# Weight tiles at six further distances from the moving operands, within 256 bytes

## The chip, the cores and the metric

The kernel runs on one core of one Trainium2 chip. The metric is the device time of one launch in microseconds, the median of several runs. Beside it stands one profiled execution with its span, from its first to its last instruction.

## The reference

One layer of a decoder trunk over 1024 tokens of width 2048, in float32:

```
h   = rmsnorm(x) * g_pre
u   = h @ w_in                      # 2048 x 7184: q, k, v, gates of two head groups
o1  = gated linear attention, 4 heads, chunked; rmsnorm per head; * silu(gate)
o2  = stick-breaking attention, 8 heads, strictly causal; * silu(gate)
x   = x + rmsnorm(concat(o1, o2) @ w_out) * g_post
x   = x + sigmoid(x @ w_g + b_g) * (p @ w_p)
```

Nearly all of the arithmetic is in three dense products: with `w_in` (2048 x 7184), `w_out` and `w_g` (2048 x 2048 each).

## The kernel before

Everything is kept transposed: features lie on the 128 partitions, tokens along the free dimension. A dense product has a weight block of 128 x 128 as TensorE's stationary operand and 128 x 512 of activations (half the tokens) as the moving one. To be exact enough, each float32 operand is split into a high part and a low remainder (`split`: ScalarE rounds a copy, VectorE subtracts it), and each block product is three matmuls: high weights with high activations, low with high, high with low. All of these land in the same accumulator `dn` in PSUM and are issued by one helper (L101).

The *first stage* works through `w_in` in units of 128 output columns. `dense` fetches a unit's weights in four pieces with `wload`: a raw tile of 128 x 512 is loaded and split into `hi` and `lo`, from a pool `w` with four buffers for each of the two. A piece holds four blocks, used for both halves of the tokens, so it serves 4 x 2 x 3 = 24 matmuls. There are 216 pieces. Between these matmuls, pieces of the attention (the tiles s, u, X, E, st and others, with accumulators z, t and o) are put in by a list of jobs that is advanced at each step. The last ten gate units of the stage have no such jobs beside them; their results pass through tiles gu, gs, ol and oB of a pool `gates`, and are stored to `og_d`.

The *wide tiles* belong to the rest: two last gate units, then the products with `w_out` and `w_g` in a form of blocks of quarters, with sums and differences of blocks in place of some of the products. Weight tiles here are 128 x 1024: a raw tile `wr` is loaded and split by `wsplit` into `wh` and `wl`, three buffers each, in a pool `mix` that is opened where the pools `w` and `gates` are closed. A wide tile holds eight blocks and serves 8 x 3 = 24 matmuls; there are 120 of them.

The order on each engine comes from a planner that works from program order and the priorities set by `tc.high_priority`. The pools are stacked: constants, activations (`ah`, `al`, 4096 bytes each per partition), `w`, and above it the pools of the attention or the gates. A tile that lies where an older tile lay waits for that tile's last use. Small filler tiles (`gap`) stand behind the small constants, so that each weight tile and each activation tile starts at a multiple of 256 bytes within the partition. Addresses per partition: activations from 7,168, `w` from 138,240, `gates` from 158,720 with oB at 168,960 to 171,008, and in `mix` the first `wr` at 172,032.

Of the kernel before, what the change touches and what calls it, by code (L numbers as in the profile page):

```python
# [12 lines left out]
F32R = mybir.dt.float32r  # L13
# [5 lines left out]
P = 128  # L19
D = 2048  # L20
T = 1024
HT = 512
# [35 lines left out]
W = 2 * HT  # L58
# [5 lines left out]
def layer(ctx, tc, xT, w_in, w_lr, w_a2, b_a, g_pre, g_head, w_out, g_post,  # L64
# [16 lines left out]
    wpool = w_open.__enter__()  # L81
# [5 lines left out]
    def nm(base):  # L87
        serial[0] += 1
        return f"{base}_{serial[0]}"
# [21 lines left out]
    def split(hi, lo, src, eng=None):  # L111
        A.activation(hi, src, AF.Copy)  # L112
        (eng or V).tensor_tensor(lo, src, f(hi), op=ALU.subtract)  # L113
# [5 lines left out]
    turn_raw = [0]  # L119
    lo_eng = [V]  # L120

    def wload(src):
        n = src.shape[-1]
        with tc.high_priority(offset=700):
            raw = new_raw[turn_raw[0] % len(new_raw)]()
            turn_raw[0] += 1
            hi = wpool.tile([P, HT], F32R, tag="hi", name=nm("hi"))
            lo = wpool.tile([P, HT], F32R, tag="lo", name=nm("lo"))
            dma(raw[:, :n], src)
            split(hi[:, :n], lo[:, :n], raw[:, :n], lo_eng[turn_raw[0] % len(lo_eng)])  # L130
        return hi, lo
# [11 lines left out]
    def dense(wsrc, acts, halves, evac):  # L143
        out_ps = {hf: ps("dn") for hf in halves}
        for q in range(KT // 4):
            hi, lo = wload(wsrc[q])
            for kk in range(4):
                k = 4 * q + kk
                sl = slice(kk * P, (kk + 1) * P)
                for hf in halves:  # L150
                    ah, al = acts[hf][k]
                    mm(out_ps[hf], hi[:, sl], ah, k == 0, False)
                    mm(out_ps[hf], lo[:, sl], ah, False, False)
                    mm(out_ps[hf], hi[:, sl], al, False, k == KT - 1)
                if k < KT - 1:
                    step()
        for hf in halves:
            with tc.high_priority(offset=300):
                evac(hf, out_ps[hf])
        step()  # L160
# [49 lines left out]
    with tc.tile_pool(name="start", bufs=1) as sp:  # L210
# [12 lines left out]
        raws = {hf: [] for hf in HALVES}  # L223
        for q in range(4):
            w = [wload(w_in[n, q]) for n in range(2)]
            for kk in range(4):
                k = 4 * q + kk
# [512 lines left out]
    with tc.tile_pool(name="mix", bufs=1, reuse_waits="tile") as mp:  # L740
        def mt(tag, bufs, n=W, dt=F32, name=None):
            return mp.tile([P, n], dt, tag=tag, name=nm(name or tag), bufs=bufs)
# [16 lines left out]
        def staged(src):  # L759
            t = mt("ar", 3)  # L760
            dma2(t, src)
            return t
# [14 lines left out]
        def wload2(src):  # L777
            raw = mt("wr", 4)
            dma(raw, src)
            return raw  # L780

        def wsplit(raw):
            hi, lo = mt("wh", 3, dt=F32R), mt("wl", 3, dt=F32R)
            split(hi, lo, raw)
            return hi, lo

# [118 lines left out]
        for hf in (1, 0):  # L905
            if hf == 0:
                job(fill("A11", 0, plain(og_d[1])))
                job(sums_12(range(3), None, early))
            for n in range(KT - LATE_SOLO, KT):
                p = None  # L910
                for kh in HALVES:
                    with ahead():
                        raw = mt("wr", 4)
                        for q in range(2):
                            dma(part(raw, q), w_in[GATE0 + n, 2 * kh + q])
                        w = wsplit(raw)
                    p = product(x_act[hf][8 * kh:8 * kh + 8], w, p=p, last=kh == 1)
                with soon():
                    if n % 2 == 0:
                        z = mt("ev", 2)  # L920
                    V.tensor_tensor(part(z, n), p, rstd[hf], op=ALU.mult)
                    if n % 2:
                        o, g = staged(o_d[hf][n // 2]), mt("sq", 1)
                        A.activation(g, z, AF.Sigmoid)
                        V.tensor_tensor(z, z, o, op=ALU.mult)
                        V.tensor_tensor(z, z, g, op=ALU.mult)
                        dma2(og_d[hf][n // 2], z)
# [3 lines left out]
        for j in range(8):  # L931
            with ahead():
                w = wsplit(wload2(w_out[0, 0, j]))
            p = product(sets["A11"], w)
            with soon():
                A.activation(u(j), p, AF.Copy)
                if j % 2:
                    dma2(m_d[j // 2], st_u[j // 2])
# [3 lines left out]
        for j in range(8):  # L942
            with ahead():
                b11, t1, t2 = (wload2(w_out[kh, nh, j]) for kh, nh in ((0, 0), (0, 1), (1, 1)))
                sub(t1, t1, b11)
                sub(t2, t1, t2)
                w2, w1 = wsplit(t2), wsplit(t1)
                add(b11, b11, t2)
                dma(t2_d[j], t2)
                dma(t3_d[j], b11)  # L950
            p = product(sets["S2"], w2)
            with soon():
                add(u(j), p, u(j))
            p = product(sets["S1"], w1)
            with soon():
                add(v(j), p, u(j))
# [267 lines left out]
```

## Time and profile before

| | |
|---|---|
| median of 3 runs | 2147.19 us (2143.7 to 2147.61) |
| the profiled execution | 2148.85 us, its span 2147.1 us |
| TensorE busy with matmuls | 2111.7 us (98%) |
| TensorE busy with weight loads | 1746.6 us (81%) |
| VectorE, ScalarE, GpSimd busy | 1372.7, 831.1, 106.7 us |
| share of the chain that ended last: matmuls into `dn` | 67% |
| bytes moved by DMA | 300.38 MB, 140 GB/s on average |

PE in the views is TensorE with its matmuls, PEld its weight loads, which run beside them. Matmuls are pipelined, so that the length of one in the profile is longer than the time from one start to the next. "L101" is line 101 of the kernel, and "dn<-ah,hi" says that the tile dn is written from ah and hi. The chain of waits goes back from the last instruction, at each step to what released it.

### The profile page before, as it was taken

The numbers are of one execution on the slowest core, as the hardware profiler recorded it, in microseconds if no ns is written. First come the engines' busy times: TensorE is split into PE (matmuls) and PEld (weight loads), VectorE is DVE, ScalarE is ACT, GpSimd is POOL, SyncE is SP. The second block draws the span as 40 slices with busy tenths as digits, with TensorE's granted clock in tenths as the row PEclk, the third lists the DMA queues.
The fourth block names the chain that finished last, engine by engine and source line by source line (L and its number), as shares of the span: only waits on it lengthen the run. The fifth ranks groups of instructions, "written<-read, shape, count | busy, mean of one in ns | idle before, by whom it ended". The sixth has DMA issues, their size and how long they took to land.

```text
span 2147.1 us, 26863 instructions
## 1 busy us (share of the span) xinstructions
PE 2111.7 (98%) x9904; PEld 1746.6 (81%) x9904; DVE 1372.7 (64%) x2147; ACT 831.1 (39%) x1347; POOL 106.7 (5%) x228
## 2 busy tenths in 40 slices
PE   9999999999999999999999999979999999999998
PEld 6788888888888888888888888868788888778787
DVE  8557676766666666666666232336777787886665
ACT  7333333333455454544544111123233443432332
POOL 3000000000101110110110000000000000000000
PEclk9999999999999999999999999989999999999999
DMA  6222221222233333333334333258887686786663
GB/s 205 73 54 56 59 61 59 55 60 55 62 86 89 75 89 88 89 81 78 93 102 120 94 98 98 87 174 311 312 319 251 219 312 205 271 286 219 223 206 123
DMA packets 215844, 300.38 MB, mean 140 GB/s; under 512 B 122913, under 2 KB 127905, under 8 KB 215713
## 3 DMA queue, kind: packets, MB, share of 16 engines
q1 hardware_dynamic: 215712, 298.67, 44.5%
q8 instruction: 77, 1.26, 0.2%
q14 instruction: 55, 0.44, 0.1%
HBM read 215.25 MB, written 56.10 MB: 126 GB/s over the span
## 4 chain that ended last, share of the span: by engine, by line
PE 77%; DMA 10%; DVE 8%; issue 2%; ACT 2%; SPq 0%; DVEq 0%; POOL 0%; ACTq 0%
PE dn L101 67%; PE z L101 5%; DMA wr<-w_g 3%; PE t L101 2%; PE o L101 2%; DVE wl L113 2%; DMA E<-X 1%; DMA ar<-h_d 1%; DMA ar<-og_d 1%; DMA wr<-w_out 1%; DVE ev L772 1%; DVE al L113 1%; DVE wr L772 1%; ACT ah L112 0%; DMA ar<-c_d 0%
## 5 line engine op out<-in xcount | busy, mean ns | idle before, releaser
L101 PE MATMUL dn<-ah,hi 128*128 128x512 f32 x1728 | 686.2, 397 | 0.2 <-ACT u L679 0.2
L101 PE MATMUL dn<-al,hi 128*128 128x512 f32 x1728 | 674.4, 390 | 0.9 <-DVE al L238 0.9
L101 PE MATMUL dn<-ah,lo 128*128 128x512 f32 x1728 | 673.8, 390 | 0.0
L101 PE MATMUL dn<-ah,wh 128*128 128x512 f32 x960 | 375.6, 391 | 11.0 <-ACT wh L112 11.0
L101 PEld LDWEIGHTS dn<-ah,hi 128*128 128x128 f32 x1728 | 325.0, 188 | 71.5 <-issue 3.6
L101 PEld LDWEIGHTS dn<-al,hi 128*128 128x128 f32 x1728 | 324.3, 188 | 72.2 <-DVE al L238 2.6
L101 PE MATMUL dn<-ah,wl 128*128 128x512 f32 x960 | 375.4, 391 | 3.5 <-DVE wl L113 3.5
L101 PE MATMUL dn<-al,wh 128*128 128x512 f32 x960 | 374.7, 391 | 0.0
L101 PEld LDWEIGHTS dn<-ah,lo 128*128 128x128 f32 x1728 | 325.2, 188 | 60.1
L112 ACT ACTIVATE hi<-raw 128x512 fp32r<-128x512 f32 x216 | 135.6, 628 | 304.5 <-PE dn L101 301.8
L113 DVE TENSOR_TENSOR lo<-raw,hi 128x512 fp32r<-128x512 f32 x216 | 150.3, 697 | 154.9 <-ACT hi L112 154.4
L101 PEld LDWEIGHTS dn<-ah,wh 128*128 128x128 f32 x960 | 181.4, 189 | 49.8 <-ACT wh L112 11.5
L101 PEld LDWEIGHTS dn<-ah,wl 128*128 128x128 f32 x960 | 181.5, 189 | 42.3 <-DVE wl L113 4.5
L101 PEld LDWEIGHTS dn<-al,wh 128*128 128x128 f32 x960 | 181.0, 189 | 37.5
L112 ACT ACTIVATE wh<-wr 128x1024 fp32r<-128x1024 f32 x120 | 126.0, 1055 | 186.7 <-PE dn L101 116.4
L113 DVE TENSOR_TENSOR wl<-wr,wh 128x1024 fp32r<-128x1024 f32 x120 | 145.8, 1218 | 18.3 <-ACT wh L112 17.8
L320 ACT ACTIVATE X<-E 128x256 uint16<-128x256 uint16 (+2 forms) x96 | 81.0, 844 | 128.5 <-DVE E L595 117.2
L590 DVE TENSOR_TENSOR_SCAN X<-X 128x128 f32<-128x128 f32 (+2 forms) x96 | 98.1, 1021 | 37.1 <-POOL X L584 24.6
L605 DVE COPY v<-E 128x512 uint16<-128x512 uint16 (+1 forms) x160 | 63.6, 430 | 59.5 <-DMA E<-X 50.2
L112 ACT ACTIVATE ah<-ar 128x1024 fp32r<-128x1024 f32 x48 | 50.9, 1061 | 105.8 <-DVE ar L775 50.8
L113 DVE TENSOR_TENSOR s<-v,s 128x512 fp32r<-128x512 f32 (+1 forms) x82 | 52.3, 637 | 48.3 <-ACT s L112 46.4
L112 ACT ACTIVATE s<-v 128x512 fp32r<-128x512 f32 (+1 forms) x82 | 47.9, 584 | 74.6 <-DVE v L605 43.3
(208 smaller groups left out, 2178.3 us busy)
## 6 DMA issues: line engine op xcount, KB each, us to landing
raw<-w_in SPq DMA_DIRECT2D x216, 256.0 KB, 2.7
wr<-w_g SPq DMA_DIRECT2D x64, 512.0 KB, 4.4
wr<-w_out SPq DMA_DIRECT2D x56, 512.0 KB, 4.8
ar<-og_d SPq DMA_DIRECT2D x36, 512.0 KB, 5.4
ar<-h_d SPq DMA_DIRECT2D x36, 512.0 KB, 4.8
xraw<-xT SPq DMA_DIRECT2D x32, 256.0 KB, 4.4
o_d<-o SPq DMA_DIRECT2D x32, 256.0 KB, 2.0
t_d<-wr SPq DMA_DIRECT2D x16, 512.0 KB, 3.2
```

What stands on the lines that cost most here:

```text
L101: PE.matmul(o, lhsT, rhs, start=start, stop=stop)
L112: A.activation(hi, src, AF.Copy)
L113: (eng or V).tensor_tensor(lo, src, f(hi), op=ALU.subtract)
L320: A.activation(pl.rearrange("p (two n) -> p two n", two=2), src.bitcast(U16)[:, :2 * n].rearrange("p (n two) -> p two n", two=2), AF.Copy)
L590: V.tensor_tensor_scan(rev, rev, rev, initial=kq[:, n:n + 1], op0=ALU.mult, op1=ALU.bypass)
L605: V.tensor_copy(to[:, :, :m, j], w[:, :, 2 * g:2 * g + m])
L772: V.tensor_tensor(dst, a, b, op=ALU.add)
```

## The change

The weight tiles of both kinds get 64 more elements (256 bytes) per partition, and the part that is used begins some elements into the tile. In the first stage it is 24, 40, 4 and 8 elements in turn (96, 160, 16 and 32 bytes), for the wide tiles 0, 8 and 32 in turn (0, 32 and 128 bytes). The high and the low tile of a pair begin at the same offset. The activations stay where they are, so the offset is also the distance of the weights from the moving operands within 256 bytes.

```diff
         with tc.high_priority(offset=700):
             raw = new_raw[turn_raw[0] % len(new_raw)]()
             turn_raw[0] += 1
-            hi = wpool.tile([P, HT], F32R, tag="hi", name=nm("hi"))
-            lo = wpool.tile([P, HT], F32R, tag="lo", name=nm("lo"))
+            o = (8, 24, 40, 4)[turn_raw[0] % 4]
+            hi = wpool.tile([P, HT + 64], F32R, tag="hi", name=nm("hi"))[:, o:o + HT]
+            lo = wpool.tile([P, HT + 64], F32R, tag="lo", name=nm("lo"))[:, o:o + HT]
             dma(raw[:, :n], src)
...
+        turn_w = [0]
+
         def wsplit(raw):
-            hi, lo = mt("wh", 3, dt=F32R), mt("wl", 3, dt=F32R)
+            o = (0, 8, 32)[turn_w[0] % 3]
+            turn_w[0] += 1
+            hi, lo = (mt(t, 3, W + 64, F32R)[:, o:o + W] for t in ("wh", "wl"))
             split(hi, lo, raw)
             return hi, lo
```

## The prediction

> **What bounds the kernel now.** The page comes first: the span, the busy times by engine, the granted clock by slice.
>
> ```profile
> span 2147.1 us, 26863 instructions
> PE 2111.7 (98%) x9904; PEld 1746.6 (81%) x9904; DVE 1372.7 (64%) x2147; ACT 831.1 (39%) x1347; POOL 106.7 (5%) x228
> PEclk9999999999999999999999999989999999999999
> ```
>
> TensorE is busy for 98% of the span at a clock that falls in one slice only. A busy TensorE is not yet a fast one, since its matmuls overlap. So the second view is the groups of instructions with their counts and lengths:
>
> ```profile
> L101 PE MATMUL dn<-ah,hi 128*128 128x512 f32 x1728 | 686.2, 397 | 0.2 <-ACT u L679 0.2
> L101 PE MATMUL dn<-ah,wh 128*128 128x512 f32 x960 | 375.6, 391 | 11.0 <-ACT wh L112 11.0
> L101 PEld LDWEIGHTS dn<-ah,hi 128*128 128x128 f32 x1728 | 325.0, 188 | 71.5 <-issue 3.6 <-ACT ah L237 3.4 <-ACT hi L112 2.5
> L101 PE MATMUL t<-s,u 128*128 128x256 f32 x288 | 43.3, 282 | 0.0
> ```
>
> The group "ah, hi" of 1728 has two sisters of the same count (al with hi, ah with lo), so the first stage has 3 x 1728 = 5184 of these matmuls; "ah, wh" of 960 stands likewise for 3 x 960 = 2880 of the wide tiles. The sum is 8064. A length of 391 ns is not the price of one. The price is the pitch, from one start to the next, and the chain of waits gives it, where "x999" matmuls follow one another with nothing between:
>
> ```profile
> 1181.44 2.75 PE dn L101 x12
> 1184.19 0.71 PE t L101 x6
> 1184.90 226.48 PE dn L101 x999
> ```
>
> 226.48 us / 999 = 226.7 ns for 512 columns. 8064 x 226.7 ns = 1828 us, 85% of the span. The kernel is bound by this pitch, and each nanosecond of it on all 8064 is 8.1 us (0.4%). What else ends waits (loads at the borders between stages, 11 us before the first wide matmul) the change touches in one place only, told below.
>
> Two more readings say what the pitch is made of. First, the six matmuls of 256 columns above take 0.71 / 6 = 118.3 ns each, with the same 128 x 128 weight load. 512 columns cost 226.7 - 118.3 = 108.4 ns more than 256, so 512 columns stream in 216.8 ns, and 9.9 ns of each pitch go with the matmul and its weight load, not with its columns. The second is the timeline of TensorE in the first stage, just after other matmuls have come in between (columns: start us, length us):
>
> ```profile
> 303.19 0.47 PE L101 MATMUL dn<-ah,hi 128*128 128x512 f32 x1
> 303.50 0.39 PE L101 MATMUL dn<-ah,lo 128*128 128x512 f32 x1
> 303.73 0.39 PE L101 MATMUL dn<-al,hi 128*128 128x512 f32 x1
> ...
> 304.88 0.39 PE L101 MATMUL z<-E,ones_r 128*128 128x512 f32 x1
> 305.11 0.39 PE L101 MATMUL dn<-ah,hi 128*128 128x512 f32 x1
> ...
> 307.15 0.39 PE L101 MATMUL dn<-ah,hi 128*128 128x512 f32 x1
> 307.38 0.39 PE L101 MATMUL dn<-ah,lo 128*128 128x512 f32 x1
> ```
>
> From 303.50 to 305.11 are seven steps, 1.61 / 7 = 230.0 ns each; from 305.11 to 307.38 are ten, 2.27 / 10 = 227.0 ns. All of them have 512 columns and one weight load, no wait is shown, and weights and moving operands start on multiples of 256 bytes. So the pitch is no constant: after a disturbance it is 3.3 ns above the settled value, and it settles within some seven matmuls. How the stream of the moving operand and the load of the next weights lie to each other in time does count. Whether their distance in memory counts too, no row shows, for every pair of the 8064 has distance 0.
>
> **The change part by part.**
>
> *The weights' start.* In the first stage all 216 pairs of hi and lo start 96, 160, 16 or 32 bytes later, 54 pairs each, and so all 5184 matmuls get a distance they did not have. Of the 120 wide pairs a third keeps 0, a third gets 32 and a third 128: 40 x 24 = 960 matmuls stay, 1920 move. Together 7104 move. No instruction is added or removed; the price is 7104 times the change of pitch. From below the bound is the 9.9 ns: if a distance took away all that goes with the weight load, 7104 x 9.9 = 70 us would be gained. From above I take the same amount once more, 70 us lost, since a load that got in the way twice as often would cost that. Between the two I take the row nearest to a pair out of step, 230.0 ns: 7104 x 3.3 ns = 23.4 us more. The reason for that sign is that the settled 226.7 is the best stretch on the chain, and what was seen at another relation of the two streams is slower. A milder form is that each new tile disturbs the pitch and it settles again: 336 tiles, all 216 + 120, x 7 steps x 3.3 ns = 7.8 us.
>
> *The weight load itself.* It lasts 188 ns and is due every 226.7, so it has 38 ns of cover; taken at nothing. If a displaced load took over 38 ns longer, each nanosecond beyond would be 7.1 us.
>
> *The splits.* ScalarE writes hi, VectorE reads it and writes lo, now at the shifted start.
>
> ```profile
> L112 ACT ACTIVATE hi<-raw 128x512 fp32r<-128x512 f32 x216 | 135.6, 628 | 304.5 <-PE dn L101 301.8 <-DMA raw<-w_in 2.0
> L113 DVE TENSOR_TENSOR wl<-wr,wh 128x1024 fp32r<-128x1024 f32 x120 | 145.8, 1218 | 18.3 <-ACT wh L112 17.8
> L113 DVE TENSOR_TENSOR s<-v,s 128x512 fp32r<-128x512 f32 x50 | 34.5, 689 | 32.7 <-ACT s L112 32.4
> L595 DVE TENSOR_TENSOR E<-E,X 128x512 f32<-128x512 f32 x48 | 33.0, 687 | 2.8 <-ACT E L580 0.7
> 1530.00:1692.00 162.00, 161.81 (x707) 133.58 (x708) 123.63 (x125) 55.89 (x54) 0.00 (x0) 0.99 0.81 281
> ```
>
> L595 reads one operand from 4 bytes past its start and takes 687 ns, where the unshifted L113 takes 689: a shifted read costs nothing. For a shifted write there is no row. I take nothing, and between -2% and +5% (0.06 us on 1218 ns, 7 us over 120) as the bound, hidden either way: in the first stage ScalarE waits 301.8 us for TensorE to free a buffer, and in the densest wide stretch (the last row: PE, PEld, DVE, ACT) VectorE is busy for 123.6 of 162 us. If that cover were gone the 7 us would show.
>
> *The loads.* The raw tiles stay where they are, so no transfer gets another target, and SyncE's queue keeps its order.
>
> *The room.* Eight buffers grow by 256 bytes in the first stage's pool (2048), six in the last one (1536). All multiples of 256 remain; what follows is moved as a block. One neighbour changes, at the border to the wide tiles. The gates' tiles lie above the first stage's pool and move up by 2048 bytes; the last pool starts below it and its first raw buffer lies as before. In layout order oB ended 1024 bytes below that buffer (171,008 against 172,032) and now reaches 1024 bytes into it. The chain there reads:
>
> ```profile
> 1414.60 1.98 DMA og_d<-oB
> 1416.63 0.04 issue
> 1416.67 0.70 DVE oB L725
> 1417.39 0.32 SPq L726
> 1417.71 0.05 issue
> 1417.76 0.42 SPq L915
> 1418.19 0.05 issue
> 1418.24 3.63 DMA wr<-w_in
> 1412.00:1428.00 16.00, 4.50 (x11) 3.17 (x11) 6.94 (x9) 4.43 (x5) 0.00 (x0) 0.58 0.59 205
> ```
>
> The first wide load goes out at 1417.76, right behind the last store of oB (1417.39). Now it has to wait until that store has landed: 1.98 us after its issue, by the first row, so 1419.4. Behind it in SyncE's queue stand the other raw loads, and the first split and matmul behind those. That is 1.6 us on the path. The clock in that stretch is 0.58, and a later restart moves the return of the full clock a little either way; I leave that at nothing.
>
> **The sum.** The profiled execution took 2148.85 us (span 2147.1 and 1.75 around it); the median of three runs is 2147.19, 1.66 lower, and the fastest 2143.7. 2148.85 + 23.4 + 1.6 = 2173.9; on the scale of the median 2172 us, 1.2% slower. A measurement of this kernel tells about 0.2% (4.3 us) from no change.
>
> **The rivals.** *The distance means nothing.* Only the 1.6 us at the border stay: 2149 us, no change. For it speaks that the pitch is the same 226.7 with many different buffers; against it, that the timeline shows a pitch that depends on how the two streams lie to each other. The Trainium skill, page "SBUF — State Buffer", section "Who interferes with whom", has this as a rule: TensorE reads moving operand and weights through two independent ports and waits for no one. By that rule the kernel would come out at 2149 us; the unequal pitches of 230 and 227 ns with nothing else waiting do not sit well with it, but no row here excludes it.
>
> *A distance takes the two reads out of each other's way, and it is faster.* The place is the 9.9 ns in each pitch, which may well be there because all pairs start at the same place within 256 bytes. With half of it gone on half of the moved matmuls: 7104 / 2 x 4.95 ns = 17.6 us less, 1.6 more at the border, 2131 us. With half of it gone on all, 2114 us. It decides from a mean pitch of 0.23 ns under 226.7 (1.6 us / 7104), and can be measured from 0.83 ns under. Against it stands that the first stage's pitch is never seen to settle below 226.7.
>
> *The pitch settles at every distance, but anew for each tile.* Then 7.8 + 1.6 us: 2157 us, slower still, by 0.4%.
>
> **How the numbers follow.** A lasting loss on most of the six distances 0.40 (2164 to 2215 us), settling anew 0.12 (2152 to 2162), nothing but the border 0.20 (2145 to 2151), a gain 0.28 (2100 to 2143). So slower 0.52, same 0.20, faster 0.28. The likeliest has its own range of 2164 to 2215. The range of all reaches from 2120 to 2206 and leaves out 0.08 at either end: half of the 9.9 ns gone on nearly all tiles below, over 8 ns more on each pitch above.
>
> **What would show it.** In the trace after, matmuls over one tile in the long run of the gates (x999 in the chain) should have a pitch that goes by the tile's distance: four values that take turns in groups of 24. Right is a mean near 230 ns there, a third of the wide tiles still at 226.7, and 188 ns for the weight load unchanged. A pitch of 226.7 in all four groups proves the first rival, any group below 226 the second, a group that starts high and ends at 226.7 the third. The first wide load should go out 1.6 us after the last store of oB rather than right behind it. The splits should stay at 628 and 1218 ns. I would be wrong most easily if one or two distances were far better or worse than the rest, since a mean of 3.3 ns hides that.

## The result and the profile after

The changed kernel takes 2182.65 us (median of 4, 2181.28 to 2184.41) against 2147.4 us (median of 4, one run more than in the table above): a ratio of 1.0159, with an interval of 1.0128 to 1.019. It is slower by 35 us. The profiled execution took 2183.27 us, its span is 34.5 us longer. From the page of the changed kernel, the span, the busy times, two groups of matmuls, a weight load and the splits:

```profile
span 2181.6 us, 26865 instructions
PE 2150.2 (99%) x9904; PEld 1750.0 (80%) x9904; DVE 1374.9 (63%) x2147; ACT 834.4 (38%) x1347; POOL 110.4 (5%) x228
L101 PE MATMUL dn<-ah,hi 128*128 128x512 f32 x1728 | 693.1, 401 | 0.2 <-ACT u L680 0.2
L101 PE MATMUL dn<-ah,wh 128*128 128x512 f32 x960 | 379.6, 396 | 11.9 <-ACT wh L112 11.9
L101 PEld LDWEIGHTS dn<-al,hi 128*128 128x128 f32 x1728 | 324.6, 188 | 78.5 <-DVE al L239 1.6
L112 ACT ACTIVATE hi<-raw 128x512 fp32r<-128x512 f32 x216 | 135.8, 629 | 329.1 <-PE dn L101 326.9
L113 DVE TENSOR_TENSOR wl<-wr,wh 128x1024 fp32r<-128x1024 f32 x120 | 145.9, 1219 | 29.2 <-ACT wh L112 24.2
```

The page hardly tells where the time went. TensorE was 98% busy and is 99% busy; a matmul grew from 397 to 401 ns in the first stage and from 391 to 396 ns in the wide part by this column, while the weight load kept its 188 ns and the splits came within 1 ns of theirs (629 and 1219, before 628 and 1218). What did grow is a wait of another engine: ScalarE now waits 326.9 us, before 301.8, for TensorE to free a weight tile. TensorE does the same work more slowly, and the clock is not the reason: its granted share is 0.994 on average in both traces.

The chain of waits shows how much more slowly, in the same unbroken run of 999 matmuls as before (columns: start us, length us):

```profile
1202.16 233.18 PE dn L101 x999
```

233.18 / 999 = 233.4 ns from start to start, against 226.7. The tiles can be told apart in TensorE's timeline, since each serves 24 matmuls; these are the first matmuls of five tiles in a row in the first stage, with the distances 32, 96, 160, 16 and 32, and of four wide tiles, with 0, 32, 128 and 0:

```profile
1251.02 0.39 PE L101 MATMUL dn<-ah,hi 128*128 128x512 f32 x1
...
1256.61 0.39 PE L101 MATMUL dn<-ah,hi 128*128 128x512 f32 x1
...
1262.22 0.39 PE L101 MATMUL dn<-ah,hi 128*128 128x512 f32 x1
...
1267.82 0.40 PE L101 MATMUL dn<-ah,hi 128*128 128x512 f32 x1
...
1273.42 0.39 PE L101 MATMUL dn<-ah,hi 128*128 128x512 f32 x1
...
1605.43 0.39 PE L101 MATMUL dn<-ah,wh 128*128 128x512 f32 x1
...
1610.88 0.39 PE L101 MATMUL dn<-ah,wh 128*128 128x512 f32 x1
...
1616.47 0.39 PE L101 MATMUL dn<-ah,wh 128*128 128x512 f32 x1
...
1622.04 0.39 PE L101 MATMUL dn<-ah,wh 128*128 128x512 f32 x1
```

Divided by 24, the first stage has 232.9, 233.8, 233.3 and 233.3 ns; the wide tiles have 5.45 / 24 = 227.1 ns at distance 0, then 232.9 at 32 and 232.1 at 128. The one distance that stayed is the one that kept its pitch.

At the border to the wide tiles the first load waits as forecast. The first line is from the kernel before, the others are from the changed one:

```profile
1411.40 0.71 DVE gu L721 x2
...
1435.36 1.39 DVE L722 TENSOR_TENSOR gu<-dn,rstd 128x512 f32<-128x512 f32 x2 [15.76 <-PE dn L101]
1443.47 3.66 SPq L920 DMA_DIRECT2D wr<-w_in  x8
1447.88 0.79 PE L101 MATMUL dn<-ah,wh 128*128 128x512 f32 x1 [11.85 <-ACT wh L112]
```

It goes out 8.11 us after VectorE takes up the last product, where it was 6.36 us (1411.40 to 1417.76). TensorE's idle time in front of the first wide matmul grew by 0.8 us only (11.85 against 11.04), because the load came in sooner once it was out.

By the starts of the first and last matmul of each part, in both traces: the first stage grew by 23.3 us (1404.1 to 1427.4), the border by 0.8, the wide part by 9.6 (717.6 to 727.2). What comes before the first of these matmuls grew by 0.6.

In the first stage some 4580 of the steps lead straight from one matmul into dn to the next, behind another of the same kind. Together they grew by 24.0 us, from 227.9 to 233.0 ns each. All other steps of that stage, around the attention's matmuls, took 360.5 us before and 359.8 after. In the wide part some 2780 such steps grew by 11.3 us, and the rest of it took 1.7 us less.

### The profile page after: what moved, and what is told of

Same layout as the page of the kernel before. It is cut to its first block, busy times and chain, and to the rows that moved or that the text cites. A ratio compares the mean times of both kernels' runs of the same rounds, so it can differ in the third digit from the quotient of the medians.

```text
span 2181.6 us, 26865 instructions
## 1 busy us (share of the span) xinstructions
PE 2150.2 (99%) x9904; PEld 1750.0 (80%) x9904; DVE 1374.9 (63%) x2147; ACT 834.4 (38%) x1347; POOL 110.4 (5%) x228
## 4 chain that ended last, share of the span: by engine, by line
PE 84%; DMA 8%; DVE 5%; issue 2%; ACT 1%; SPq 1%; DVEq 0%; ACTq 0%
PE dn L101 73%; PE z L101 6%; PE t L101 2%; PE o L101 2%; DMA wr<-w_g 1%; DVE wl L113 1%; DMA ar<-h_d 1%; DMA ar<-og_d 1%; DVE al L113 1%; DMA xraw<-xT 1%; DMA ar<-xT 1%; DMA ar<-c_d 1%; ACT ah L112 0%; DMA wr<-w_out 0%; DMA t_d<-wr 0%
## 5 line engine op out<-in xcount | busy, mean ns | idle before, releaser
L101 PE MATMUL dn<-ah,lo 128*128 128x512 f32 x1728 | 683.5, 396 | 0.0
L101 PE MATMUL dn<-al,hi 128*128 128x512 f32 x1728 | 682.0, 395 | 0.5 <-DVE al L239 0.4
L101 PE MATMUL dn<-ah,wh 128*128 128x512 f32 x960 | 379.6, 396 | 11.9 <-ACT wh L112 11.9
L101 PE MATMUL dn<-al,wh 128*128 128x512 f32 x960 | 379.3, 395 | 0.0
L112 ACT ACTIVATE hi<-raw 128x512 fp32r<-128x512 f32 x216 | 135.8, 629 | 329.1 <-PE dn L101 326.9
L113 DVE TENSOR_TENSOR wl<-wr,wh 128x1024 fp32r<-128x1024 f32 x120 | 145.9, 1219 | 29.2 <-ACT wh L112 24.2
```

The costliest lines, as they stand in the source:

```text
L101: PE.matmul(o, lhsT, rhs, start=start, stop=stop)
```

## The experiments

The theory from here on is called *distance*: while one matmul streams its moving operand, the weights of the next one are loaded, and the place of the two within 256 bytes decides how much they hold each other up. Its rivals: *layout* (the padding, or what it moved), *settling* (a new distance from tile to tile disturbs a pitch that would settle), *alignment* (a tile off a multiple of 256 is slow by itself).

**Only the padding.**

```diff
-            o = (8, 24, 40, 4)[turn_raw[0] % 4]
+            o = (0, 0, 0, 0)[turn_raw[0] % 4]
-            o = (0, 8, 32)[turn_w[0] % 3]
+            o = (0, 0, 0)[turn_w[0] % 3]
```

> The changed kernel with all offsets 0: the tiles keep their 256 bytes of padding, so the layout and the overlap at the border to the wide tiles are the changed kernel's, but every distance is 0. Distance theory (the distance between the weights that are loaded and the operand that streams sets the pitch): the long run of 999 matmuls returns to 226.7 ns each (226.5 us), and what is left is the border, so the time is 1 to 2 us above the kernel before, about 2148 us. Layout theory (the padding or what it moved is slow): it stays near 2180 us, with 233 ns in the long run.

Measured: 2149.93 us against 2147.59, a ratio of 1.0007 (0.9998 to 1.0016). Its chain has the old pitch again:

```profile
1186.22 226.48 PE dn L101 x999
```

Layout is out, and in the measured time the cost of the border cannot be told from nothing.

**One distance for all.**

```diff
-            o = (8, 24, 40, 4)[turn_raw[0] % 4]
+            o = (8, 8, 8, 8)[turn_raw[0] % 4]
-            o = (0, 8, 32)[turn_w[0] % 3]
+            o = (8, 8, 8)[turn_w[0] % 3]
```

> Every weight tile at distance 32, none changes its distance from tile to tile. Distance theory: 233 ns on all 8064, 233.1 us for the long run; against the changed kernel the 960 wide matmuls at distance 0 lose 5.6 ns each (5.4 us), the first stage stays, so about 2187 us. Settling theory (each tile with a new distance disturbs the pitch, and it settles again): nothing is disturbed any more, 226.7 ns in the long run and 2150 us.

Measured: 2187.77 us, a ratio of 1.0187 (1.0171 to 1.0202), within a microsecond of what the distance theory gave. The chain:

```profile
1205.10 233.11 PE dn L101 x999
```

233.3 ns, although nothing changes from tile to tile. Settling is out: at distance 32 the pitch stays where it is.

**Both operands moved.** The kernel before, with the activations and everything above them 32 bytes further on:

```diff
-        gap(const, 224)
+        gap(const, 256)
```

> The kernel before with 32 more bytes of filler behind the constants, so activations and weights both start 32 bytes past a multiple of 256 and the distance between them stays 0. Distance theory: 226.7 ns in the long run, 2147 us, as before. Alignment theory (a weight tile or a moving operand that does not start at a multiple of 256 is slow by itself): 233 ns, 2180 to 2190 us.

Measured: 2154.02 us, a ratio of 1.0031 (1.002 to 1.0041). In its trace the pitch has not changed:

```profile
1186.78 226.48 PE dn L101 x999
```

Alignment is out as the cause of the 35 us. The 0.3% that remain are not in the pitch of the matmuls into `dn`, which is 226.7 ns in the wide part as well (2778 starts). Their cause stays open: the shift also moves every tile above the constants that a DMA loads or stores, and it gives a distance of 32 or 224 bytes to the few matmuls that take one operand from the constants.

**Each half of the change alone.** First stage with the wide tiles at 0, and the reverse:

```diff
first_only:
-            o = (0, 8, 32)[turn_w[0] % 3]
+            o = (0, 0, 0)[turn_w[0] % 3]
wide_only:
-            o = (8, 24, 40, 4)[turn_raw[0] % 4]
+            o = (0, 0, 0, 0)[turn_raw[0] % 4]
```

> The change in the first stage alone (96, 160, 16, 32); wide tiles padded, at distance 0. If the pitch of each matmul is all there is, the parts add up: the first stage of the changed kernel ends 24 us later than before, the border stays, so 2147.5 + 24 + 1 = about 2172 us.

> The change in the wide tiles alone (0, 32, 128); the first stage padded, at distance 0. 960 matmuls at 233.0 and 960 at 232.2 instead of 226.8 are 11.1 us; with the border about 2159 us if nothing beside the matmuls hides it. If the loads and sums of the wide stages hide a part, less than that: 2153 to 2157.

Measured: 2172.23 us, a ratio of 1.012 (1.0103 to 1.0136), and 2155.85 us, 1.0036 (1.0022 to 1.0049). The two excesses over 1 add up to 1.56%, and the whole change has 1.59%. The wide half came out at the lower of its two expectations: its matmuls alone should have cost 11.1 us, and 8.3 were seen. In its trace the steps from one matmul into dn to the next grew by 11.9 us in the wide part, and the rest of that part, the steps around other matmuls and the waits, took 4.9 us less: it takes up a part of the loss.

**Only the low weights moved.**

```diff
-            o = (8, 24, 40, 4)[turn_raw[0] % 4]
+            o = (0, 0, 0, 0)[turn_raw[0] % 4]
-            lo = wpool.tile([P, HT + 64], F32R, tag="lo", name=nm("lo"))[:, o:o + HT]
+            lo = wpool.tile([P, HT + 64], F32R, tag="lo", name=nm("lo"))[:, 8:8 + HT]
...
-            hi, lo = (mt(t, 3, W + 64, F32R)[:, o:o + W] for t in ("wh", "wl"))
+            hi, lo = (mt(t, 3, W + 64, F32R)[:, s:s + W] for t, s in (("wh", 0), ("wl", 8)))
```

> High weight tiles at distance 0, low ones at 32, in both stages, so two of three matmuls have distance 0. Order in the first stage: high weights with high activations, low with high, high with low. If what counts is the operand that streams against the weights that are being loaded for the next matmul: the first of the three, beside which low weights are loaded, takes about 235 ns, the other two 225 to 228. If what counts is the distance of a matmul's own weights: the second is the slow one. Either way a mean of 229 to 230 ns and about 2168 us; a mean of 226.7 would say that a single displaced load can be made good in the next matmul.

Measured, in one run: 2189.46 us. The expectation of the time was wrong: with two thirds of the matmuls at distance 0 the kernel is as slow as with none. Chain and timeline:

```profile
1203.53 233.10 PE dn L101 x999
```

```profile
1252.36 0.40 PE L101 MATMUL dn<-ah,hi 128*128 128x512 f32 x1
1252.60 0.39 PE L101 MATMUL dn<-ah,lo 128*128 128x512 f32 x1
1252.83 0.40 PE L101 MATMUL dn<-al,hi 128*128 128x512 f32 x1
1253.06 0.40 PE L101 MATMUL dn<-ah,hi 128*128 128x512 f32 x1
```

The longest step follows the start of "ah, hi". Means over all starts of the trace with a neighbour of the same kind (wide tiles): 239.2 ns from "ah, wh" to "ah, wl" (915), 228.2 from there to "al, wh" (946), 232.6 to the next "ah, wh" (917). The matmul that is held up most is not the one whose own weights lie at 32, it is the one that streams while these are being loaded. That is the distance theory. The load itself does not get longer in the profile: 189 ns for the low weights of the wide tiles, as before. What the theory had not foreseen is the 232.6: the matmul two steps on, with both distances at 0, does not return to 226.7. The three together take 700.0 ns, 3 x 233.3.

**Other distances.** Three kernels with the padding and other lists of offsets (in bytes: 48, 64, 80, 112 and 144, 176, 192; then 208, 224, 240, 256 and 4, 64, 252 with 512 bytes of padding; then 8, 12, 20, 24 and 236, 244, 248):

```diff
-            o = (8, 24, 40, 4)[turn_raw[0] % 4]
-            o = (0, 8, 32)[turn_w[0] % 3]
scan_a:
+            o = (12, 16, 20, 28)[turn_raw[0] % 4]
+            o = (36, 44, 48)[turn_w[0] % 3]
scan_b:
+            o = (52, 56, 60, 64)[turn_raw[0] % 4]
+            o = (1, 16, 63)[turn_w[0] % 3]
scan_c:
+            o = (2, 3, 5, 6)[turn_raw[0] % 4]
+            o = (59, 61, 62)[turn_w[0] % 3]
```

> Seven further distances: 48, 64, 80, 112 in the first stage, 144, 176, 192 for the wide tiles. If every distance but 0 is alike: pitches of 231 to 235 ns on each, about 2190 us (no wide tile at 0 any more). If only some distances are in the way of the stream: one or more of the seven at 226.7 or below. A distance below 226 ns would be worth a kernel of its own.

> Distances 208, 224, 240 and 256 in the first stage, 4, 64 and 252 for the wide tiles (buffers padded by 512 bytes). If 256 bytes are the period: 226.7 ns at 256, 231 to 234 at 208, 224 and 240, and 64 as slow in the wide stages as it was in the first one (233.4). 4 and 252 tell how sharp the good place is: 226.7 if some bytes do not matter, 231 to 235 if only a start in step counts. Any distance under 226 would be worth a kernel.

> Small distances on both sides of 0: 8, 12, 20, 24 in the first stage, 236, 244, 248 for the wide tiles. From 4 (232.3), 16 (231.8), 240 (228.5) and 252 (232.4 ns): 231 to 234 at the first four, 228 to 233 at the last three. Any under 226 would make a faster kernel; I expect none. Time about 2185 us.

Measured, one run each: 2179.31, 2169.25 and 2178.63 us; the first and the last are 11 and 6 us less than expected. The pitch by distance, each the mean over 880 to 1140 starts of the trace, for 0 over 2785 and 4575 (one matmul into `dn` after another, both at that distance, the first one after other matmuls and steps over 330 ns left out; 16, 32, 96, 128 and 160 are from the changed kernel):

| bytes | ns | bytes | ns | bytes | ns |
|---|---|---|---|---|---|
| 0 (wide, padding alone) | 226.8 | 64 (first, wide) | 233.4, 233.6 | 208 | 232.0 |
| 4 | 232.3 | 80 | 231.7 | 224 | 233.1 |
| 8 | 230.8 | 96 | 233.8 | 236 | 231.7 |
| 12 | 231.3 | 112 | 233.4 | 240 | 228.5 |
| 16 | 231.8 | 128 | 232.2 | 244 | 232.9 |
| 20 | 232.8 | 144 | 231.9 | 248 | 233.3 |
| 24 | 231.1 | 160 | 233.6 | 252 | 232.4 |
| 32 | 233.0 | 176 | 230.4 | 256 (first) | 228.2 |
| 48 | 233.3 | 192 | 231.8 | 0 (first, padding alone) | 227.9 |

256 behaves as 0 does in the same stage, 64 the same in both stages. Three came out under the range expected for them, 176, 8 and 240; 248 came out 0.3 ns over its range. 0 is best, 240 comes next, and 4 bytes to either side are enough to lose it. Not one lies under 226.7 ns.

**Low weights at other distances.** The high tiles at 0 and the low ones at 240, 176, 128, 208 and, for the wide tiles, 16, 80, 144:

```diff
-            hi = wpool.tile([P, HT + 64], F32R, tag="hi", name=nm("hi"))[:, o:o + HT]
+            hi = wpool.tile([P, HT + 64], F32R, tag="hi", name=nm("hi"))[:, 0:HT]
-            o = (8, 24, 40, 4)[turn_raw[0] % 4]
+            o = (60, 44, 32, 52)[turn_raw[0] % 4]
...
-            o = (0, 8, 32)[turn_w[0] % 3]
+            o = (4, 20, 36)[turn_w[0] % 3]
-            hi, lo = (mt(t, 3, W + 64, F32R)[:, o:o + W] for t in ("wh", "wl"))
+            hi, lo = (mt(t, 3, W + 64, F32R)[:, s:s + W] for t, s in (("wh", 0), ("wl", o)))
```

> High weight tiles at 0, low ones at 240, 176, 128 and 208 in the first stage, at 16, 80 and 144 for the wide tiles. Question: is any mean over the three matmuls of a block under 226.7 ns, as single steps of 224 were? Expected from the low tiles at 32 (239, 228, 233 in turn): the matmul beside which the low weights are loaded differs from its neighbours at each, and the mean is 226.7 or 233.3, or between them where it does not settle; none below 226. Time 2165 to 2185 us.

Measured, one run: 2162.55 us, a little under the range expected. Means over the three matmuls of a block: 227.8 ns at 240, 231.0 at 176, 231.4 at 128, 231.1 at 208, 228.5 at 16, 231.3 at 80, 229.4 at 144. Again none under 226.7, so no version was found that beats the kernel before.

## Why the prediction was right, and where it was off

Direction and mechanism held. The forecast was 2172 us, measured were 2182.65; the likeliest case had 2164 to 2215 us. Part of this is luck. The row under the price, 230.0 ns, has its operands at distance 0: it shows that the pitch depends on how the two streams lie to each other in time, and nothing of their place in memory. That the second counts too was a choice between open cases (0.40 for a lasting loss), and nothing made a size taken from the first fit it.

- *The price per matmul was too small.* The step is the term 7104 x 3.3 ns = 23.4 us. It was sized by a row where the pitch was on its way back to 226.7 (230.0 ns). At a distance that lasts the pitch has no way back: 231.8 to 233.8 ns at the five new distances (they are six only if 32 is counted once for each stage). For the wide tiles that is 5.8 ns on average over their 226.8 (233.0 and 232.2). In the first stage it is 5.2 ns over 227.9, since other matmuls disturb the pitch there all the time and it was above its settled value before. The term also counts all 5184 matmuls of that stage, while the growth is all in the some 4580 steps straight from one to the next. Measured: 23.3 us in the first stage and 9.6 in the wide part, 32.9 in place of 23.4.
- *The border* was forecast at 1.6 us. The load goes out 1.75 us later, as said, but it lands sooner and TensorE waits only 0.8 us longer. In the ten traces with padded tiles the time from the start of the last matmul of the first stage to that of the first wide one is 12.2 to 12.8 us, in the two without padding 11.4. The term was right in kind; 0.8 to 1.4 us of the 1.6 were seen.
- *The loads.* That no transfer gets another target holds for the raw tiles alone: the tiles above the first stage's pool, which have loads and stores too, moved by 2048 bytes. With the padding alone this cost nothing that the time shows.
- *The splits and the weight load* at nothing: right, to within 1 ns: 188 for the load, 629 and 1219 for the splits.
- *A third of the wide tiles at 226.7*: right, with 227.1 in the rows and 227.5 over 883 starts, the disturbance at each change included.
- *The rivals.* That distance means nothing is refuted by the pitch per tile and by the padding alone. That each tile settles anew is refuted by the kernel with one distance for all. That a distance takes the two reads out of each other's way is refuted for the 24 other distances tried. 32 bytes between the two operands, with nothing else changed, cost 6.6 ns of each matmul in the long run. The Trainium skill, "SBUF — State Buffer", section "Who interferes with whom", says that TensorE's two read ports are independent and that it waits for no one. The runs do not bear this out, and where on the way from memory the two get into each other's way, none shows.

The bound that was taken as the best case, 9.9 ns per matmul to be gained, remains unreached. Whether it can be reached by other means was not tried.

## What to carry to other kernels

Where float32 matmuls like these (128 x 128 weights, 512 columns, a weight load each) follow one another without a gap, look at the time from start to start and not at the length in the profile; two tiles that are streamed and loaded side by side should have the same place within 256 bytes, weights of the next matmul against the operand of this one. One kind of tile out of step can be enough to lose all of it, as the low weights at 32 bytes did; at 240 bytes they lost nothing (227.8 ns against 227.9 in that stage) and at 16 bytes 1.7 ns. A price read from a passing disturbance was too low for one that lasts: 3.3 ns against 5.2 and 5.8.

## What the runs showed of the hardware

The settled pitch lies on a beat. In the trace of the kernel before, the 4987 starts with a settled pitch (behind seven steps of 226 or 227 ns) lie on one beat of 6.67 ns: in stretches of 100 us their phases agree (mean vector of 0.95 to 0.97, where 1 is exact). A run without a break would agree with any whole part of its pitch. But in the first 1200 us, where other matmuls break in all the time, a 33rd or a 35th part of 226.7 ns gives only 0.11 to 0.72.

226.7 ns are 34 of these beats, and 233.3 are 35. With all weights at 32, and with the low ones alone at 32, the long run has 233.3 ns each. At 32 the steps are 232 and 235 in turn, at 160 they are 231, 238 and 231, at 96 they go round in seven; after each change of distance they reach their cycle within some matmuls. These cycles close on whole beats: two steps of 466.7 ns together (70 beats), three of 700.0 (105), seven of 1640.0 (246), as means from the tenth step of a tile on. The mean of one step need not be a whole number: at 176 four steps take 920.1 ns (138 beats), which is 34.5 for each. At others, 16 and 128 among them, no cycle shows within the 24 matmuls of a tile.

With the low weights alone at 32 the three steps of a block take 105 beats, where they took 102. Why a third of the loads, displaced, costs as much as all of them, and what the beat is, no run here tells.
